# One 128-feature group of a down-projection: the moving operand of 288 columns split into two of 144, each with its own weight load

## The chip, the cores and the metric

The kernel runs on one core of a Trainium2 chip. The metric is the device time of one execution in microseconds (us); lower is better. Before the change three runs took 1708.25, 1707.87 and 1704.91 us: a median of 1707.87 us.

Names used below: PE is TensorE's matmul stream, PEld its weight loads (a record LDWEIGHTS for every record MATMUL), DVE is VectorE, ACT is ScalarE, POOL is GpSimd, SP is the SyncE queue that starts the weight transfers. The weights are the stationary operand of a matmul, the activations the moving one; "288 columns" is the width of the moving operand, and so of the output row in PSUM.

## The reference, cut to what matters

The reference is one layer of a decoder: a combined input projection, a gated convolution, a gated delta rule, an output projection with a layer norm, then a feed-forward block with a second layer norm. The change lies in the last product of the feed-forward block:

```
hid = jnp.square(jax.nn.relu(x @ w_up))          # 2048 -> 8192 features
x = layer_norm(ALPHA * x + hid @ w_down, ln2_g, ln2_b)   # 8192 -> 2048
```

There are 256 prompt tokens and 8 x 4 sample tokens, 288 in all. They are handled together: everything is kept with the features on the 128 partitions and the 288 tokens along the free dimension.

## The kernel before, in words

**Products.** All weights and activations are fp32. Each is split into a high and a low part of type float32r, and a product is three matmuls into the same PSUM columns: high weights by high activations (line 206), high weights by low activations (line 207), low weights by high activations (line 208). Each of the three comes with a load of a 128x128 tile of weights, and then streams 288 columns. Line 207 uses the same weights as line 206 and still has its own load.

**Groups and blocks.** `add_group` lists the work as groups of output features. A group is normally 256 features (two tiles of 128), and is cut into blocks of 4 x 128 rows by 256 columns of weights, 512 KB. A block passes four stages: `load` starts its transfer on SP, `split_hi` (ACT, line 179) makes the high part, `split_lo` (DVE, line 186, recorded as line 140) the low part, and `matmuls` issues its 24 matmuls on PE. The main loop at the end of the kernel goes through the blocks in order. In the step of block i it makes the high and the low part of block i + 3, runs what is due at i (the list `due`, filled by `at`), issues the matmuls of block i and starts the transfer of block i + 7. The order of each engine's queue is the order of this code.

**The end of the program.** The feed-forward block goes through four chunks of 2048 hidden features: eight groups of `w_up`, then the groups of `w_down` whose products are added into the residual `acc` in SBUF. In the last chunk the last 256 output features are two groups of 128 (`cols=P`, so that a block holds 8 x 128 rows by 128 columns, and a group of 16 row tiles is two blocks):

- the next-to-last group, features 1792 to 1919: 2 blocks, 16 row tiles, 48 matmuls. `next_to_last` adds its result to `acc` in the step of the block that follows, `collect` one block later transposes it (`turned(14)`, line 608) and gathers the layer norm's statistics of 15 of the 16 feature tiles;
- the last group, features 1920 to 2047: also 48 matmuls. Then `final` adds the result, turns the last tile, finishes the statistics, and writes the output.

Around them on PE stand transposes of finished tiles (`out_tiles` and `turned`, line 608), put there by `at`: four ahead of the last group's first block, two ahead of its second.

The matmul's `start` flag marks the first matmul that writes a PSUM bank; the accumulation of a group lies in one bank.

Of the kernel before, what the change touches and what calls it, by code (L numbers as in the profile page):

```python
# [16 lines left out]
P = 128  # L17
D = 2048
NP_ = 256
NS = 32  # L20
NT = NP_ + NS
NX = NT + 2
KT = D // P
# [10 lines left out]
GW = 256  # L34
# [69 lines left out]
def hybrid_kernel(ctx: ExitStack, tc: tile.TileContext, A):  # L104
# [15 lines left out]
    def nm(s):  # L120
        counter[0] += 1
        return f"{s}{counter[0]}"
# [13 lines left out]
    act, dve, pe, gps, sp = nc.scalar, nc.vector, nc.tensor, nc.gpsimd, nc.sync  # L136
# [11 lines left out]
    w_in = A["w_in"][0]  # L148
    blocks = []

    def add_group(W, col0, row0, nk, acts, evac, width=NT, cols=GW):
        kb = KB * GW // cols
        gi = dict(W=W, col0=col0, acts=acts, evac=evac, width=width, cols=cols, kb=kb)
        for j in range(nk // kb):
            blocks.append((gi, row0 + j * kb * P, j * kb, j == 0, j == nk // kb - 1))

# [4 lines left out]
    def at(i, f):  # L161
        due.setdefault(i, []).append(f)
# [25 lines left out]
    def matmuls(i):  # L188
        gi, r0, k0, first, last = blocks[i]
        if first:  # L190
            gi["ps"] = acp.tile([P, 2, 512], F32, tag="acc", name=nm("acc"))
        ps = gi["ps"]
        h, l = his.pop(i), los.pop(i)
        ah, al = gi["acts"]()
        n = gi["width"]
        kb = gi["kb"]
        h, l = (u.rearrange("p k c -> p (k c)").rearrange("p (k c) -> p k c", k=kb) for u in (h, l))
        for k in range(kb):
            for t in range(gi["cols"] // P):
                o = ps[:, t, 0:n]  # L200
                wh = h[:, k, t * P:(t + 1) * P]
                wl = l[:, k, t * P:(t + 1) * P]
                xh_, xl_ = ah[:, k0 + k, 0:n], al[:, k0 + k, 0:n]
                st = first and k == 0
                en = last and k == kb - 1
                pe.matmul(o, wh, xh_, start=st, stop=False)  # L206
                pe.matmul(o, wh, xl_, start=False, stop=False)  # L207
                pe.matmul(o, wl, xh_, start=False, stop=en)  # L208
                if fill:
                    fill.pop(0)()  # L210
        if last:
            for n, f in enumerate(gi["evac"]):
                at(i + 1 + n, lambda f=f: f(ps))
# [83 lines left out]
    for G in range(2):  # L297
        mark["kqv", G] = len(blocks)
        for sec, c0 in ((1, C_K), (0, C_Q), (2, C_V)):
            for p in range(2):  # L300
                add_group(w_in, c0 + 512 * G + GW * p, 0, KT, acts_x, conv_evac(sec, G, p))
        mark["kqv_end", G] = len(blocks)
# [46 lines left out]
    for p in range(4):  # L349
        add_group(w_in, C_H + GW * p, 0, KT, acts_x, h_evac(p))  # L350
        add_group(w_in, C_GC + GW * p, 0, KT, acts_x, gc_evac(p))
        add_group(w_in, C_GB + GW * p, 0, KT, acts_x, gb_evac(p))
# [399 lines left out]
    for c in range(4):  # L752
# [4 lines left out]
        acts_h = lambda: (ph["hh"], ph["hl"])  # L757
        for p in range(8 if c < 3 else 7):
            add_group(A["w_down"][0], GW * p, 2048 * c, KT, acts_h, down_evac(c, p))

    add_group(A["w_down"][0], D - 2 * P, 3 * 2048, KT, acts_h, [next_to_last, collect], cols=P)
    add_group(A["w_down"][0], D - P, 3 * 2048, KT, acts_h, [final], cols=P)


# [574 lines left out]
    t = raw.pop(0)  # L1339
# [16 lines left out]
    for i in range(3):  # L1356
        split_hi(i + 1, 2)
        split_lo(i + 1, 2)
        load(i + 5)
        fill.extend(lambda k=k: x_tile(k) for k in range(4 * i + 4, 4 * i + 8))  # L1360
        matmuls(i)
# [9 lines left out]
    for i in range(3, len(blocks)):  # L1371
# [47 lines left out]
        if i == mark["down3"] - 60:  # L1419
            tail_consts()  # L1420
        matmuls(i)
        load(i + AHEAD + 4)
    for i in sorted(due):
# [31 lines left out]
```

## Time and profile before

| | |
|---|---|
| device time, median of 3 runs | 1707.87 us (1704.91 to 1708.25) |
| profiled execution: span from its first to its last instruction | 1703.4 us |
| difference of the median and that span | 4.5 us |
| PE busy / weight loads busy | 1688.5 us / 1668.7 us, 13063 records each |
| DVE / ACT / POOL busy | 1007.2 / 734.1 / 133.8 us |
| matmuls of 288 columns by 128x128 float32r weights: busy, mean | 295 to 300 ns |
| their weight loads: busy, mean | 188 to 189 ns |

The page gives the profiled execution's span and no other time of it; what lies around the span is told only by the 4.5 us to the median of the runs.

How to read it: matmuls are pipelined, so that the "busy" duration of one (295 ns) is its way through the array and not what it costs. What it costs is the distance from its start to the start of the next. In the rows of a timeline the first number is the start in us from the begin of the span, the second the duration in us of the row (of all of its instructions from the first start to the last end, where "x4" or "x16" stands at the end), then engine, source line, operation, output and inputs, the tile (128*128 is a weight tile of 128 rows and 128 columns) and the moving operand.

### The profile page before, as it was taken

How to read it: one execution, taken by the hardware profiler on the slowest of the kernel's cores; microseconds unless marked ns; L12 is line 12 of the kernel's file. 1: busy time of each engine (PE TensorE's matmuls, PEld its weight loads, DVE VectorE, ACT ScalarE, POOL GpSimd, SP SyncE). 2: the span in 40 equal slices, each digit the busy share in tenths (PEclk: the TensorE clock that was granted, in tenths of full speed). 3: DMA queues.
4: the chain of work that ended last, by engine and by line, in shares of the span. 5: the costliest groups of instructions: out<-in, count | busy, mean ns of one | idle time of the engine just before them, and what ended most of it. 6: DMA issues, size and time to landing. Idle time of an engine off the chain costs nothing.

```text
span 1703.4 us, 31106 instructions
## 1 busy us (share of the span) xinstructions
PE 1688.5 (99%) x13063; PEld 1668.7 (98%) x13063; DVE 1007.2 (59%) x1296; ACT 734.1 (43%) x1067; POOL 133.8 (8%) x223
## 2 busy tenths in 40 slices
PE   9999999999999999999999999999999999999997
PEld 7999999999999999999999999999999999999997
DVE  5577876758544444456778844566445654466565
ACT  4675626333543333334445533444334433344442
POOL 2232412023300000000010000000000000000000
PEclk9999999999999999999999999999999999999999
DMA  8464456435555555555565555555555555555552
GB/s 244 140 194 139 123 175 200 150 115 180 162 170 169 166 162 170 163 164 165 158 190 174 165 170 161 164 170 162 167 168 161 163 171 162 164 167 164 162 162 80
DMA packets 275097, 279.18 MB, mean 164 GB/s; under 512 B 13131, under 2 KB 270092, under 8 KB 274952
## 3 DMA queue, kind: packets, MB, share of 16 engines
q1 hardware_dynamic: 270414, 265.95, 51.3%
q0 software_dynamic: 4256, 11.12, 2.3%
q8 instruction: 102, 1.67, 0.4%
q14 instruction: 37, 0.30, 0.1%
q10 hardware_dynamic: 288, 0.13, 0.0%
HBM read 269.68 MB, written 7.48 MB: 163 GB/s over the span
## 4 chain that ended last, share of the span: by engine, by line
PE 98%; DVE 1%; DMA 0%; POOL 0%; issue 0%; SPq 0%; ACT 0%; POOLq 0%; ACTq 0%
PE acc L206 31%; PE acc L208 31%; PE acc L207 31%; PE g L1084 1%; DMA xr<-in_x_prompt_dram 0%; PE g L1072 0%; PE g L1231 0%; PE g L1251 0%; PE g L831 0%; DVE w L143 0%; PE g L1254 0%; PE g L1203 0%; PE g L1243 0%; PE g L608 0%; PE g L798 0%; PE g L958 0%
## 5 line engine op out<-in xcount | busy, mean ns | idle before, releaser
L140 DVE TENSOR_TENSOR lo<-raw,hi 128x1024 fp32r<-128x1024 f32 (+2 forms) x502 | 614.0, 1226 | 556.2 <-ACT hi L179 553.7
L179 ACT CAST hi<-raw 128x1024 fp32r<-128x1024 f32 (+1 forms) x498 | 517.6, 1041 | 765.0 <-PE acc L207 707.7
L206 PE MATMUL acc<-xh,hi 128*128 128x288 f32 x1408 | 422.9, 300 | 0.0
L208 PE MATMUL acc<-xh,lo 128*128 128x288 f32 x1408 | 416.7, 296 | 0.0
L207 PE MATMUL acc<-xl,hi 128*128 128x288 f32 x1408 | 416.5, 296 | 0.0
L206 PE MATMUL acc<-dh,hi 128*128 128x290 f32 x1024 | 303.9, 297 | 0.0
L207 PE MATMUL acc<-dl,hi 128*128 128x290 f32 x1024 | 303.3, 296 | 0.0
L208 PE MATMUL acc<-dh,lo 128*128 128x290 f32 x1024 | 302.7, 296 | 0.0
L206 PE MATMUL acc<-hh,hi 128*128 128x288 f32 x1024 | 302.3, 295 | 0.0
L208 PE MATMUL acc<-hh,lo 128*128 128x288 f32 x1024 | 302.3, 295 | 0.0
L207 PE MATMUL acc<-hl,hi 128*128 128x288 f32 x1024 | 302.3, 295 | 0.0
L206 PEld LDWEIGHTS acc<-xh,hi 128*128 128x128 f32 x1408 | 265.4, 189 | 2.6 <-issue 0.7
L207 PEld LDWEIGHTS acc<-xl,hi 128*128 128x128 f32 x1408 | 265.8, 189 | 0.5
L208 PEld LDWEIGHTS acc<-xh,lo 128*128 128x128 f32 x1408 | 265.6, 189 | 0.0
L206 PEld LDWEIGHTS acc<-dh,hi 128*128 128x128 f32 x1024 | 193.6, 189 | 0.1
L208 PEld LDWEIGHTS acc<-dh,lo 128*128 128x128 f32 x1024 | 193.3, 189 | 0.0
L207 PEld LDWEIGHTS acc<-dl,hi 128*128 128x128 f32 x1024 | 193.3, 189 | 0.1
L207 PEld LDWEIGHTS acc<-hl,hi 128*128 128x128 f32 x1024 | 192.5, 188 | 0.0
L208 PEld LDWEIGHTS acc<-hh,lo 128*128 128x128 f32 x1024 | 192.3, 188 | 0.0
L206 PEld LDWEIGHTS acc<-hh,hi 128*128 128x128 f32 x1024 | 192.1, 188 | 0.0
L207 PE MATMUL acc<-ml,hi 128*128 128x288 f32 x256 | 75.6, 295 | 0.0
L208 PE MATMUL acc<-mh,lo 128*128 128x288 f32 x256 | 75.6, 295 | 0.0
(404 smaller groups left out, 1620.0 us busy)
## 6 DMA issues: line engine op xcount, KB each, us to landing
raw<-in_w_in_dram SPq DMA_DIRECT2D x176, 512.0 KB, 3.5
raw<-in_w_up_dram SPq DMA_DIRECT2D x128, 512.0 KB, 3.9
raw<-in_w_down_dram SPq DMA_DIRECT2D x128, 512.0 KB, 3.7
raw<-in_w_o_dram SPq DMA_DIRECT2D x32, 512.0 KB, 3.7
raw<-in_w_a_out_dram SPq DMA_DIRECT2D x16, 512.0 KB, 3.7
raw<-in_w_b_out_dram SPq DMA_DIRECT2D x16, 512.0 KB, 3.6
S<-in_state_gdn_dram POOLq DMA_DIRECT2D x8, 512.0 KB, 7.8
out_dram<-S POOLq DMA_DIRECT2D x8, 512.0 KB, 4.9
```

The source lines that it names most:

```text
L140: dve.tensor_tensor(out=out, in0=a, in1=b, op=op)
L179: act.copy(his[i][:, k:k + step], raw[i][:, k:k + step])
L206: pe.matmul(o, wh, xh_, start=st, stop=False)
L207: pe.matmul(o, wh, xl_, start=False, stop=False)
L208: pe.matmul(o, wl, xh_, start=False, stop=en)
L1084: pe.matmul(out[r, q * 64:q * 64 + 64], a[r, q, :], b[r, q, :], start=True, stop=True)
```

## The change

`add_group` gets an argument `parts`, kept with the group. `matmuls` runs the three matmuls of a weight tile once for each part, over a slice of the 288 columns. All groups have `parts=1`, one part of 288 columns as before, and only the next-to-last group has `parts=2`: columns 0 to 143 first, all three matmuls, then columns 144 to 287. So its 48 matmuls of 288 columns become 96 of 144, and its weight loads 96 instead of 48. The `start` flag is set on the very first matmul of the group alone, whose bank holds both halves. `skip_group_check=True` tells the builder not to check the nesting of the flags; it adds no instruction.

```diff
-    def add_group(W, col0, row0, nk, acts, evac, width=NT, cols=GW):
+    def add_group(W, col0, row0, nk, acts, evac, width=NT, cols=GW, parts=1):
...
-                o = ps[:, t, 0:n]
                 wh = h[:, k, t * P:(t + 1) * P]
                 wl = l[:, k, t * P:(t + 1) * P]
-                xh_, xl_ = ah[:, k0 + k, 0:n], al[:, k0 + k, 0:n]
-                st = first and k == 0
                 en = last and k == kb - 1
-                pe.matmul(o, wh, xh_, start=st, stop=False)
-                pe.matmul(o, wh, xl_, start=False, stop=False)
-                pe.matmul(o, wl, xh_, start=False, stop=en)
+                for u in range(gi["parts"]):
+                    cs = slice(u * n // gi["parts"], (u + 1) * n // gi["parts"])
+                    o = ps[:, t, cs]
+                    xh_, xl_ = ah[:, k0 + k, cs], al[:, k0 + k, cs]
+                    st = first and k == 0 and u == 0
+                    pe.matmul(o, wh, xh_, start=st, stop=False, skip_group_check=True)
+                    pe.matmul(o, wh, xl_, start=False, stop=False, skip_group_check=True)
+                    pe.matmul(o, wl, xh_, start=False, stop=en, skip_group_check=True)
...
-    add_group(A["w_down"][0], D - 2 * P, 3 * 2048, KT, acts_h, [next_to_last, collect], cols=P)
+    add_group(A["w_down"][0], D - 2 * P, 3 * 2048, KT, acts_h, [next_to_last, collect], cols=P, parts=2)
```

The changed code is two lines longer above the functions that follow, so lines 206, 207, 208 and 608 are 208, 209, 210 and 610 after it. The instructions of DVE, ACT, POOL and SP, and their order, are the same; PE's are the same outside this group.

The first place is PE's queue where the group begins: the last two matmuls of the group before (acc2038), and the first of the next-to-last group (acc2051). hh and hl are the high and low activations, hi and lo the parts of a weight block. Before:

```order
L207 MATMUL acc2038_17553<-hl1832_15784,hi2036_17548 128x288
L208 MATMUL acc2038_17553<-hh1831_15783,lo2037_17550 128x288
L206 MATMUL acc2051_17686<-hh1831_15783,hi2040_17580 128x288 [waits PE_49]
L207 MATMUL acc2051_17686<-hl1832_15784,hi2040_17580 128x288
L208 MATMUL acc2051_17686<-hh1831_15783,lo2041_17582 128x288 [waits DVE_49]
L206 MATMUL acc2051_17686<-hh1831_15783,hi2040_17580 128x288
```

And after the change:

```order
L209 MATMUL acc2038_17553<-hl1832_15784,hi2036_17548 128x288
L210 MATMUL acc2038_17553<-hh1831_15783,lo2037_17550 128x288
L208 MATMUL acc2051_17686<-hh1831_15783,hi2040_17580 128x144 [waits PE_49]
L209 MATMUL acc2051_17686<-hl1832_15784,hi2040_17580 128x144
L210 MATMUL acc2051_17686<-hh1831_15783,lo2041_17582 128x144 [waits DVE_49]
L208 MATMUL acc2051_17686<-hh1831_15783,hi2040_17580 128x144
```

The matmuls are half as wide, the waits stand at the same two, and the sixth row is no longer the next row tile but the second half of the first.

The second place is PE's queue where the group ends: its last matmuls, the four transposes of finished tiles (g2052, g2053) and the first matmul of the last group (acc2054). Before:

```order
L208 MATMUL acc2051_17686<-hh1831_15783,lo2043_17610 128x288
L608 MATMUL g2052_17735<-cf_75,acc_9588 128x128 [waits DVE_49]
L608 MATMUL g2052_17735<-cf_75,acc_9588 128x128
L608 MATMUL g2053_17741<-cf_75,acc_9588 128x128 x2
L206 MATMUL acc2054_17748<-hh1831_15783,hi2046_17649 128x288 [waits PE_49,Activation_49]
```

And after the change:

```order
L210 MATMUL acc2051_17686<-hh1831_15783,lo2043_17610 128x144
L610 MATMUL g2052_17783<-cf_75,acc_9588 128x128 [waits DVE_49]
L610 MATMUL g2052_17783<-cf_75,acc_9588 128x128
L610 MATMUL g2053_17789<-cf_75,acc_9588 128x128 x2
L208 MATMUL acc2054_17796<-hh1831_15783,hi2046_17649 128x288 [waits PE_49,Activation_49]
```

What follows the group is the same, with the same waits, 48 instructions later.

More of the change, by code (lines that the diff above doesn't have):

```diff
@@ L149, in hybrid_kernel @@
     blocks = []
-    def add_group(W, col0, row0, nk, acts, evac, width=NT, cols=GW):
+    def add_group(W, col0, row0, nk, acts, evac, width=NT, cols=GW, parts=1):
         kb = KB * GW // cols
-        gi = dict(W=W, col0=col0, acts=acts, evac=evac, width=width, cols=cols, kb=kb)
+        gi = dict(W=W, col0=col0, acts=acts, evac=evac, width=width, cols=cols, kb=kb, parts=parts)
         for j in range(nk // kb):
```

## The prediction

> **What bounds the kernel now.** I read the page first: the span, the row of each engine, the clock, and the shares of the chain that ended last.
>
> ```profile
> span 1703.4 us, 31106 instructions
> PE 1688.5 (99%) x13063; PEld 1668.7 (98%) x13063; DVE 1007.2 (59%) x1296; ACT 734.1 (43%) x1067; POOL 133.8 (8%) x223
> ...
> PEclk9999999999999999999999999999999999999999
> ...
> PE 98%; DVE 1%; DMA 0%; POOL 0%; issue 0%; SPq 0%; ACT 0%; POOLq 0%; ACTq 0%
> ```
>
> TensorE is the bound: 98% of the chain, at the full clock. Both of its rows, streams and loads, are nearly full, so the rows do not say which of the two limits. That is read from the distances between starts in the timeline. This is PE where the group begins and ends.
>
> ```profile
> 1674.49 0.30 PE L208 MATMUL acc<-hh,lo 128*128 128x288 f32 x1
> 1674.63 0.29 PE L206 MATMUL acc<-hh,hi 128*128 128x288 f32 x1
> ...
> 1680.89 0.29 PE L208 MATMUL acc<-hh,lo 128*128 128x288 f32 x1
> 1681.02 0.60 PE L608 MATMUL g<-cf,acc 128*128 128x128 f32 x4
> ```
>
> The group is the 48 matmuls from 1674.63 to 1681.02 (the four transposes at 1681.02 are the row of line 608 that follows it in the queue): 6.39 us, 0.1331 us each, without a gap. The busy time of that stretch, by engine (PE, PEld, DVE, ACT, POOL, then clock and DMA share):
>
> ```profile
> 1674.63:1681.02 6.39, 6.39 (x50) 6.39 (x49) 1.89 (x2) 1.25 (x3) 0.00 (x0) 1.00 0.01 3
> ```
>
> DVE and ACT work 1.89 and 1.25 us of it, the DMA share is 0.01: all weights are there. The chain behind the last matmul of the program, from the chain in order of time:
>
> ```profile
> 1688.09 0.15 PE acc L208
> 1688.26 0.43 DVE acc L140
> 1688.74 0.45 PE g L608 x2
> ...
> 1697.16 1.30 POOLq L1451
> ```
>
> It hangs on the last matmul of the last group (1688.09). Whatever the group adds on PE moves this end by as much.
>
> **The change, part by part.** What it removes: 48 matmuls of 288 columns, 6.39 us. What it adds: 96 matmuls of 144 columns and 96 loads of 128x128 weights. Nothing moves on another engine. No row of the trace has a float32r matmul of 144 columns, so its price comes from two separate ones: what 144 columns take to stream, and what a load takes when the stream no longer covers it. The larger of the two is the distance.
>
> The stream first. Two matmuls of 512 columns (line 997), the next matmul behind them, and sixteen of 288 columns over weights of only 32 columns (line 831), with the matmul behind them:
>
> ```profile
> 300.43 0.63 PE L997 MATMUL g<-glx,hmr 128*128 128x512 f32 x2
> 300.90 0.29 PE L206 MATMUL acc<-xh,hi 128*128 128x288 f32 x1
> ...
> 45.13 2.27 PE L831 MATMUL g<-xh,wba 128*32 128x288 f32 x16
> 47.23 0.30 PE L206 MATMUL acc<-xh,hi 128*128 128x288 f32 x1
> ```
>
> 512 columns take (300.90 - 300.43) / 2 = 0.235 us, 0.459 ns a column; 288 columns take 0.1331, 0.462 ns a column. With a quarter of the weights to load, 288 columns still take (47.23 - 45.13) / 16 = 0.131. So today the stream sets the distance and the load lies under it. 144 columns at 0.462 ns are 0.0665 us.
>
> The load next. In the gates there is a run of matmuls with full 128x128 weights and streams of 8 to 64 columns, too short to cover anything (loads first, then three of their streams):
>
> ```profile
> 72.25 0.30 PEld L873 LDWEIGHTS g<-be,ao 128*128 128x128 f32 x2
> 72.48 0.30 PEld L874 LDWEIGHTS g<-g,cf 128*128 128x128 f32 x2
> 72.70 0.30 PEld L875 LDWEIGHTS g<-gm,cf 128*128 128x128 f32 x2
> 72.92 0.30 PEld L876 LDWEIGHTS g<-be,ao 128*128 128x128 f32 x2
> 73.15 0.30 PEld L877 LDWEIGHTS g<-be,ao 128*128 128x128 f32 x2
> 73.37 0.30 PEld L878 LDWEIGHTS g<-be,ao 128*128 128x128 f32 x2
> 73.59 0.19 PEld L206 LDWEIGHTS acc<-xh,hi 128*128 128x128 f32 x1
> 73.70 0.19 PEld L207 LDWEIGHTS acc<-xl,hi 128*128 128x128 f32 x1
> ...
> 72.28 0.37 PE L873 MATMUL g<-be,ao 128*128 128x16 f32 x2
> 72.73 0.41 PE L875 MATMUL g<-gm,cf 128*128 128x64 f32 x2
> 73.17 0.37 PE L877 MATMUL g<-be,ao 128*128 128x8 f32 x2
> ```
>
> Twelve loads from 72.25 to 73.59: 1.34 us, 0.1117 each, whether 8 or 64 columns stream. These weights are plain fp32. That float32r weights cost the same is seen at the two loads behind them: the one of line 206 starts at 73.59 and the next at 73.70, 0.11 later. The same stands where the last group begins, behind the transposes:
>
> ```profile
> 1681.35 0.19 PEld L206 LDWEIGHTS acc<-hh,hi 128*128 128x128 f32 x1
> 1681.46 0.19 PEld L207 LDWEIGHTS acc<-hl,hi 128*128 128x128 f32 x1
> 1681.60 0.19 PEld L208 LDWEIGHTS acc<-hh,lo 128*128 128x128 f32 x1
> ```
>
> There the first load found a short stream ahead of it and held the next up by 0.11; the one after it found a stream of 288 columns, and the distance was the usual 0.14. The durations agree, from the groups by line and shape (the last numbers before the second bar are the total and the mean in ns):
>
> ```profile
> L831 PEld LDWEIGHTS g<-xh,wba 128*32 128x32 f32 x16 | 1.7, 108 | 0.4
> ...
> L206 PEld LDWEIGHTS acc<-hh,hi 128*128 128x128 f32 x1024 | 192.1, 188 | 0.0
> L207 PEld LDWEIGHTS acc<-hl,hi 128*128 128x128 f32 x1024 | 192.5, 188 | 0.0
> ```
>
> 32 columns of float32r weights take 108 ns, 128 take 188: 80 ns for 96 columns, 0.83 ns a column, 107 ns for 128. The rest is latency that two loads share. The last two rows also show that line 207 loads weights that are already in the array, 1024 times of 1024: nothing drops a repeated load, so the second half's loads are paid too.
>
> The sum: 0.1117 is larger than 0.0665, so the load sets the distance. 96 x 0.1117 = 10.72 us in place of 6.39: **+4.33 us**. On the path that sets the end all of it is paid, since PE has no gap in the group or behind it that could take it up. From 1703.4 the span goes to 1707.7; the median stands 4.5 above that span, and I carry the difference over: 1707.87 + 4.33 = **1712.2 us**.
>
> Bounds of the distance: not below the stream, 0.0665, which gives 96 x 0.0665 = 6.38 and no change (a gain is excluded, since the columns streamed stay 13824; at 0.459 ns a column it would be 0.05 us). Above, with the load as long as today's distance, 0.1331: 12.78, +6.39 us. I take 0.1117, as it comes from loads of the same size under streams that cannot cover them.
>
> The Trainium skill, "TensorE: Matmul & The Clock Gate", section "LDWEIGHTS (loading the stationary operand)", gives the load as its columns divided by 1.2 GHz, 106.7 ns for 128. By that rule the group would take 96 x 0.1067 = 10.24 us, +3.85 instead of the row's +4.33. The row's 0.1117 is 5 ns longer than the rule; the trace agrees on the slope and decides on the size.
>
> Edits that cost nothing: the flags and the unchecked nesting add no instruction. The adds and transposes of finished tiles on DVE and PE come later by what PE loses; they have the last group's matmuls as cover. On DVE:
>
> ```profile
> 1681.44 0.50 DVE L610 BATCH_NORM_STATS2 r<-g 128x6 f32<-128x128 f32 x2 [3.73 <-PE g L608]
> ...
> 1685.08 0.50 DVE L610 BATCH_NORM_STATS2 r<-g 128x6 f32<-128x128 f32 x2 [1.72 <-PE g L608]
> ```
>
> DVE waits 3.73 and 1.72 us for PE around the group's end, never PE for DVE; a later PE lengthens these waits and nothing else. If that cover were gone, the 0.50 us rows would show on the path.
>
> **The rivals.**
>
> *Hidden: not slower.* The next weights are fetched while two short streams run, a second load starting before the first is in use, and the stream's 0.0665 sets the distance: 1707.9 us. For it: today's loads start a whole matmul ahead of their streams. Against it: the run at 72.25 had nothing to do but load, and still took 0.1117 each; the queue was full of loads there too. It decides if the loads' distance falls under 0.067. Chance 0.07.
>
> *Half hidden.* Only part of the load is exposed, with a distance midway between 0.0665 and 0.1117, 0.089: 8.54 us, +2.15, 1710.0 us. Against it, again, the 0.1117 for all widths from 8 to 64. The Trainium skill, same page, section "Back-to-back issue gap", measures about 81 ns for a load and a matmul of 128 columns in a stream of pairs; with 16 more columns by the 0.462 ns above, an estimate of 88 ns, +2.1 us. None of the rows above with 128x128 weights is as quick. Chance 0.07.
>
> *In turn.* Load and stream do not overlap in this pattern: 0.1117 + 0.0665 = 0.178, 17.1 us, +10.7, 1718.6 us. Against it: today 0.1331 holds a load of 0.11 and a stream of 0.133, so they overlap. The skill's page says, in "Part 3: Packing small matmuls — row/col tiling", that loads overlap matmuls in flight only with other row groups, which would mean this. The trace contradicts it in every row of the group, as all use 128 rows. Chance 0.06, with other costs above the forecast. A slower clock, because PE streams less of the time, would be one of these; in the run of short streams it stayed at 1.00 (the number behind POOL's in the row of that stretch):
>
> ```profile
> 72.00:73.60 1.60, 1.60 (x17) 1.60 (x16) 1.53 (x4) 1.58 (x3) 0.21 (x1) 1.00 0.98 317
> ```
>
> **How the numbers follow.** The forecast, a distance of 0.105 to 0.12, has 0.80. A measurement of this kernel can tell about 0.2% from no change, 3.42 us. The forecast lies 0.91 us above that, and the three runs before spread over 3.34, so the forecast alone gives "slower" in some 0.72 of its cases: 0.58. With "in turn" (0.06) and a little of "half hidden" that is 0.65. Faster has no mechanism, only the runs' spread: 0.02. Within 0.2%: 0.33.
>
> The range: at the bottom the rival without a change at today's median, 1707.8; at the top the bound of 0.1331 on the highest run, 1708.25 + 6.39 = 1714.6. What it leaves out is "in turn" and the tails of the spread, some 0.17.
>
> **What would show it.** In the profile after: 96 rows of 128x144 in the group, starts 0.11 apart on both PE and PEld, the group 10.7 us long, the chain from the last matmul to the end 15.3 us (1703.4 - 1688.1) as now, the clock row still full. Starts 0.067 apart would prove the first rival, 0.178 the third. The prediction is wrong if the group is 10.7 us long and the time has not followed, or if the group is shorter than 9.6 us.

## The result, and the profile after

| | before | after |
|---|---|---|
| device time, median | 1706.70 us (18 runs, 1704.91 to 1708.69) | 1711.03 us (18 runs, 1709.20 to 1713.52) |
| span of the profiled execution | 1703.4 us | 1707.8 us |
| the next-to-last group on PE | 6.39 us | 10.67 us |

The ratio is 1.0025, with a 95% interval of [1.0018, 1.0032]: slower by 4.33 us between the medians. Part of the spread lies outside the change: of the 18 runs after, the four with the lowest mean granted clock (0.991) took 1712.56 to 1713.52 us, the other fourteen 1709.20 to 1711.76. The page of the profile after, the same rows as before:

```profile
span 1707.8 us, 31202 instructions
...
PE 1693.1 (99%) x13111; PEld 1673.0 (98%) x13111; DVE 1007.5 (59%) x1296; ACT 734.6 (43%) x1067; POOL 134.1 (8%) x223
...
PEclk9999999999999999999999999999999999999999
```

48 matmuls and 48 loads more (13111 for 13063), both rows as full as before, the clock the same. Nothing here says where the 4.4 us of the span went; the distances in the timeline do. PE, from the last 288-column matmul ahead of the group to the transposes behind it:

```profile
1674.61 0.30 PE L210 MATMUL acc<-hh,lo 128*128 128x288 f32 x1
1674.74 0.23 PE L208 MATMUL acc<-hh,hi 128*128 128x144 f32 x1
1674.81 0.27 PE L209 MATMUL acc<-hl,hi 128*128 128x144 f32 x1
1674.91 0.28 PE L210 MATMUL acc<-hh,lo 128*128 128x144 f32 x1
...
1685.30 0.28 PE L210 MATMUL acc<-hh,lo 128*128 128x144 f32 x1
1685.41 0.61 PE L610 MATMUL g<-cf,acc 128*128 128x128 f32 x4
```

And its weight loads:

```profile
1674.61 0.19 PEld L208 LDWEIGHTS acc<-hh,hi 128*128 128x128 f32 x1
1674.74 0.19 PEld L209 LDWEIGHTS acc<-hl,hi 128*128 128x128 f32 x1
1674.85 0.19 PEld L210 LDWEIGHTS acc<-hh,lo 128*128 128x128 f32 x1
...
1685.23 0.19 PEld L210 LDWEIGHTS acc<-hh,lo 128*128 128x128 f32 x1
```

The distances between the loads hold the whole argument. The row of a matmul stands 0.06 to 0.07 us behind the row of its load (1674.74 and 1674.81, 1685.23 and 1685.30), which is what 144 columns take to stream; that is not what sets the pace. The loads start 0.11 apart from 1674.74 to 1685.23 (94 distances, 10.49 us, 0.1116 each), and from the second matmul on the matmuls start as far apart as they do. The group takes 10.67 us (1685.41 - 1674.74). The busy time of that stretch, with clock and DMA share behind the five engines:

```profile
1674.74:1685.41 10.67, 10.67 (x98) 10.67 (x97) 1.89 (x2) 1.25 (x3) 0.00 (x0) 1.00 0.01 2
```

DVE and ACT do the same 1.89 and 1.25 us of work in it as before. Behind the group the span is as long as it was: 1707.8 - 1685.41 = 22.39 us, before 1703.4 - 1681.02 = 22.38. DVE's waits around the end of the group:

```profile
1685.85 0.50 DVE L612 BATCH_NORM_STATS2 r<-g 128x6 f32<-128x128 f32 x2 [8.03 <-PE g L610]
...
1689.48 0.50 DVE L612 BATCH_NORM_STATS2 r<-g 128x6 f32<-128x128 f32 x2 [1.73 <-PE g L610]
```

The first wait for PE has grown from 3.73 to 8.03 us, by the 4.3 that PE lost; the second is as it was.

### The profile page after: what moved, and what is told of

Its sections match the earlier page's. It is cut to its first block, busy times and chain, and to the rows that moved or that the text cites. A ratio compares the mean times of both kernels' runs of the same rounds, so it can differ in the third digit from the quotient of the medians.

```text
span 1707.8 us, 31202 instructions
## 1 busy us (share of the span) xinstructions
PE 1693.1 (99%) x13111; PEld 1673.0 (98%) x13111; DVE 1007.5 (59%) x1296; ACT 734.6 (43%) x1067; POOL 134.1 (8%) x223
## 4 chain that ended last, share of the span: by engine, by line
PE 98%; DVE 1%; DMA 0%; POOL 0%; issue 0%; SPq 0%; ACT 0%; POOLq 0%; ACTq 0%
PE acc L208 31%; PE acc L210 31%; PE acc L209 31%; PE g L1086 1%; DMA xr<-in_x_prompt_dram 0%; PE g L1074 0%; PE g L1233 0%; PE g L1253 0%; PE g L833 0%; DVE w L143 0%; PE g L1256 0%; PE g L1205 0%; PE g L610 0%; PE g L1245 0%; PE g L800 0%; PE g L960 0%
## 5 line engine op out<-in xcount | busy, mean ns | idle before, releaser
L209 PE MATMUL acc<-hl,hi 128*128 128x288 f32 (+1 forms) x1040 | 306.4, 295 | 0.0
L210 PE MATMUL acc<-hh,lo 128*128 128x288 f32 (+1 forms) x1040 | 306.4, 295 | 0.0
L208 PE MATMUL acc<-hh,hi 128*128 128x288 f32 (+1 forms) x1040 | 306.3, 295 | 0.0
```

The costliest lines, as they stand in the source:

```text
L208: pe.matmul(o, wh, xh_, start=st, stop=False, skip_group_check=True)
L209: pe.matmul(o, wh, xl_, start=False, stop=False, skip_group_check=True)
L210: pe.matmul(o, wl, xh_, start=False, stop=en, skip_group_check=True)
```

## The experiments

All kernels start from the changed one. Theory A is the prediction's: the distance between two matmuls is the larger of the stream (0.462 ns a column) and the load of the next weights (0.1117 us for 128 columns). Theory B: a matmul has a fixed cost of its own, whatever it loads, some 0.09 us. Theory C: the change of the output columns costs.

### Half the weights: e1_weights64

```diff
-                wh = h[:, k, t * P:(t + 1) * P]
-                wl = l[:, k, t * P:(t + 1) * P]
+                mw = 64 if gi["parts"] > 1 else P
+                wh = h[:, k, t * P:t * P + mw]
+                wl = l[:, k, t * P:t * P + mw]
...
-                    o = ps[:, t, cs]
+                    o = ps[0:mw, t, cs]
...
-        tt(a, a, ps[:, 0, 0:NT], ADD)
+        tt(a[0:64], a[0:64], ps[0:64, 0, 0:NT], ADD)
```

> The split group loads only 64 of its 128 weight columns and leaves out output features 1856 to 1919; as many matmuls, loads and streamed columns as in the changed kernel. Theory A (the load sets the distance; 0.83 ns a weight column): a load takes some 0.058 us, the stream of 144 columns 0.0665 covers it, the 96 matmuls take 6.4 us, and the time is that of before, 1706.7 us, 4.3 under the changed kernel. Theory B (a fixed cost of each further matmul, about 0.09 us, whatever it loads): starts 0.11 apart as in the changed kernel, 10.7 us, 1711.0.

Measured: 1706.71 us (11 runs) beside 1706.15 for before, ratio 1.0004 [0.9995, 1.0013]. PE in this kernel, where a weight tile reads 128*64:

```profile
1675.43 0.23 PE L209 MATMUL acc<-hh,hi 128*64 128x144 f32 x1
1675.50 0.23 PE L210 MATMUL acc<-hl,hi 128*64 128x144 f32 x1
1675.56 0.23 PE L211 MATMUL acc<-hh,lo 128*64 128x144 f32 x1
...
1681.93 0.61 PE L611 MATMUL g<-cf,acc 128*128 128x128 f32 x4
```

The same 96 matmuls of 144 columns with 96 loads take 6.50 us (1681.93 - 1675.43), 0.0677 each, in place of 10.67. The only thing that was made smaller on PE is the weight tile, and with it the rows of the output that it makes. B is dead: the further matmuls, their issue and the halves together cost no more than 0.11 us (6.50 for the 6.39 of before); the length of the load does.

### Shorter loads, shorter streams: e7_weights64_four72

e1, and besides:

```diff
-    add_group(A["w_down"][0], D - 2 * P, 3 * 2048, KT, acts_h, [next_to_last, collect], cols=P, parts=2)
+    add_group(A["w_down"][0], D - 2 * P, 3 * 2048, KT, acts_h, [next_to_last, collect], cols=P, parts=4)
```

> Weights of 64 columns (output features 1856 to 1919 are left out) and four parts of 72 columns, so that the stream, 0.033 us, no longer covers the shorter load. Theory A: the distance is the load of 64 columns, about 0.058 us, 192 of them 11.1 us. Theory B: 0.100 apart, 19.2 us, as with full weights.

Measured: 1709.86 us in one run; the group, by the row of its stretch:

```profile
1674.50:1685.67 11.17, 11.17 (x195) 11.17 (x193) 1.89 (x2) 1.25 (x3) 0.00 (x0) 1.00 0.01 3
```

192 matmuls in 11.17 us, 0.0582 each; A had 11.1. With streams of 0.033 the load of 64 columns is bare. Beside the changed kernel there are now two bare loads, 0.0582 for 64 columns and 0.1116 for 128: 0.83 ns a column and some 5 ns besides.

### Wide and narrow: e2_256_32

```diff
-                    cs = slice(u * n // gi["parts"], (u + 1) * n // gi["parts"])
+                    cs = slice(0, n) if gi["parts"] == 1 else (slice(0, NP_), slice(NP_, n))[u]
```

> Split into 256 and 32 columns instead of 144 and 144. Theory A: a matmul of 256 columns takes its stream, 256 x 0.462 ns = 0.118 us, which covers the next load; one of 32 columns takes the next load, 0.112: 48 x 0.230 = 11.0 us. Theory B, by the line 0.0893 us and 0.152 ns a column: 0.128 and 0.094, 48 x 0.222 = 10.7 us, with the wide ones well over their stream.

Measured: 1710.67 us in one run. The loads of this kernel, from the second one of the group on, and the transposes' loads behind it:

```profile
1675.51 0.19 PEld L209 LDWEIGHTS acc<-hl,hi 128*128 128x128 f32 x1
1675.62 0.19 PEld L210 LDWEIGHTS acc<-hh,lo 128*128 128x128 f32 x1
1675.74 0.19 PEld L208 LDWEIGHTS acc<-hh,hi 128*128 128x128 f32 x1
1675.86 0.19 PEld L209 LDWEIGHTS acc<-hl,hi 128*128 128x128 f32 x1
1675.97 0.19 PEld L210 LDWEIGHTS acc<-hh,lo 128*128 128x128 f32 x1
...
1686.46 0.20 PEld L610 LDWEIGHTS g<-cf,acc 128*128 128x128 f32 x2
```

The three distances under 256 columns are 0.11, 0.12, 0.12, the one under 32 columns that follows 0.11. A had 0.118 and 0.112, B 0.128 and 0.094: the last one speaks for A. From the first row to the last, the whole group but its first load, it is 10.95 us (1686.46 - 1675.51), between A's 11.0 and B's 10.7 and close to A.

### The halves apart: e4_halves_outer

```diff
-        for k in range(kb):
+        for u, k in [(u, k) for u in range(gi["parts"]) for k in range(kb)]:
             for t in range(gi["cols"] // P):
...
-                for u in range(gi["parts"]):
```

> The same 96 matmuls, but in each block all matmuls of the first 144 columns come before all of the second, so that the half changes once a block instead of every three matmuls. Theory A: starts 0.11 apart, 10.7 us, as the loads are the same. Theory C (it is the change of the output columns that costs, 47 changes of some 0.09 us): about 6.5 us.

Measured: 1713.52 us in one run, a span of 1711.7. The row of the group's stretch:

```profile
1677.93:1688.60 10.67, 10.67 (x98) 10.67 (x97) 1.89 (x2) 1.25 (x3) 0.00 (x0) 1.00 0.01 2
```

10.67 us, to the hundredth what the changed kernel takes: theory C is out. That this one run is 2.5 us over the changed kernel's median is not the group's doing: the group begins 3.2 us later here (1677.93 for 1674.74), so the difference was there ahead of it. The granted clock shows where: between 9 and 24 us it was 0.57 here and 1.00 in the changed kernel's trace, between 210 and 230 us 0.83 and 1.00.

### Elsewhere, and more of it: e6_last_group and e5_chunk

```diff
-    add_group(A["w_down"][0], D - 2 * P, 3 * 2048, KT, acts_h, [next_to_last, collect], cols=P, parts=2)
-    add_group(A["w_down"][0], D - P, 3 * 2048, KT, acts_h, [final], cols=P)
+    add_group(A["w_down"][0], D - 2 * P, 3 * 2048, KT, acts_h, [next_to_last, collect], cols=P)
+    add_group(A["w_down"][0], D - P, 3 * 2048, KT, acts_h, [final], cols=P, parts=2)
```

> The last group is split instead of the next-to-last. Theory A: the next-to-last group takes 6.4 us, the last one's two blocks 10.7 us, and the time is that of the changed kernel, 4.3 over before, 1711.0 us. If the place counted (the transposes and adds of finished tiles as cover), it would come out more than 1 us away from that.

Measured: 1713.16 us (7 runs) beside 1706.67 for before, ratio 1.0032 [1.0020, 1.0043]. The interval holds the 1.0025 of the changed kernel, but the median lies 2.2 us above A's 1711.0, so by its own words ("more than 1 us") the expectation missed. The trace says whether the place is the reason. The next-to-last group is short again, from the first row to the second 6.40 us:

```profile
1675.62 0.29 PE L208 MATMUL acc<-hh,hi 128*128 128x288 f32 x1
...
1682.02 0.60 PE L610 MATMUL g<-cf,acc 128*128 128x128 f32 x4
```

Behind it lie 1708.6 - 1682.02 = 26.58 us, in the kernel before 22.38: the split costs 4.20 us in the last group, where it cost 10.67 - 6.39 = 4.28 in the next-to-last. So the place makes no difference of 1 us. The span is 0.8 us above the changed kernel's because the next-to-last group began 0.9 us later; between 9 and 24 us the granted clock was 0.67 here and 1.00 there. The median is high for the same reason: four of these seven runs have the mean clock of 0.991, of the changed kernel's eighteen also four; the other three took 1710.38 to 1711.34 us, A's 1711.0 within 0.7.

For e5 every group of the last chunk gets two parts:

```diff
-            add_group(A["w_down"][0], GW * p, 2048 * c, KT, acts_h, down_evac(c, p))
+            add_group(A["w_down"][0], GW * p, 2048 * c, KT, acts_h, down_evac(c, p), parts=2 if c == 3 else 1)
...
-    add_group(A["w_down"][0], D - P, 3 * 2048, KT, acts_h, [final], cols=P)
+    add_group(A["w_down"][0], D - P, 3 * 2048, KT, acts_h, [final], cols=P, parts=2)
```

> All nine groups of the last chunk of the down-projection in two halves: 768 matmuls of 288 become 1536 of 144, sixteen times the change. Theory A, with nothing to take it up anywhere: 768 x (2 x 0.1117 - 0.1331) = 69.4 us over before, 1776.1 us, ratio 1.0407. If part of the added time were taken up by waits around the group, the gain per group would be smaller in the other groups or the ratio below 1.03.

Measured: 1775.45 us beside 1706.67, ratio 1.0399 [1.0384, 1.0413]: 68.8 us for the 69.4 of A. The cost is 16 times that of one group, so over the nine groups it is paid in full. Most of that stretch, by engine:

```profile
1582.53:1750.00 167.47, 167.47 (x1506) 167.47 (x1504) 59.67 (x94) 38.07 (x50) 0.10 (x1) 1.00 0.27 83
```

### Four parts, and the clock: e3_four72

```diff
-    add_group(A["w_down"][0], D - 2 * P, 3 * 2048, KT, acts_h, [next_to_last, collect], cols=P, parts=2)
+    add_group(A["w_down"][0], D - 2 * P, 3 * 2048, KT, acts_h, [next_to_last, collect], cols=P, parts=4)
```

> Four parts of 72 columns, 192 matmuls and 192 loads. Theory A: the distance stays at the load's 0.1117, 192 x 0.1117 = 21.4 us, 15.1 over before: 1721.8 us, ratio 1.0088. Theory B, with a line through the two measured distances (0.1331 at 288 columns, 0.1112 at 144: 0.0893 us and 0.152 ns a column): 0.100 apart, 19.2 us, 12.9 over before: 1719.6.

Measured: 1738.03 us (5 runs) beside 1706.15, ratio 1.0191 [1.0178, 1.0205]: 31.9 us over before, where A had 15.1 and B 12.9. Both missed. Two stretches of the group (clock in the third column from the end), and the loads at the seam:

```profile
1675.63:1681.57 5.94, 5.94 (x56) 5.94 (x55) 1.89 (x2) 1.25 (x3) 0.00 (x0) 1.00 0.01 3
1681.57:1711.01 29.44, 29.44 (x141) 29.44 (x140) 0.00 (x0) 0.00 (x0) 0.00 (x0) 0.50 0.00 1
```

```profile
1681.43 0.19 PEld L210 LDWEIGHTS acc<-hh,lo 128*128 128x128 f32 x1
1681.55 0.29 PEld L208 LDWEIGHTS acc<-hh,hi 128*128 128x128 f32 x1
1681.71 0.34 PEld L209 LDWEIGHTS acc<-hl,hi 128*128 128x128 f32 x1
1681.93 0.33 PEld L210 LDWEIGHTS acc<-hh,lo 128*128 128x128 f32 x1
1682.14 0.33 PEld L208 LDWEIGHTS acc<-hh,hi 128*128 128x128 f32 x1
```

For 5.94 us the distance is A's 0.112. Then the granted clock falls to 0.50 and the loads stand 0.21 apart. PE is as "busy" as ever, 5.94 of 5.94 and 29.44 of 29.44. What is new is the share of the time in which columns stream: 0.033 of 0.112 us, 30%, against 0.0665 of 0.112, 60%, in the changed kernel. e7 streams the same 72 columns in as many matmuls but 0.033 of 0.058, 57%, and its clock stayed at 1.00 (its row above): neither the number nor the width of the matmuls decides by itself, and the share fits all three. e7's weight tile is half as wide, a second difference. The four runs that follow vary the share under full weights, where it changes together with the width; that it is the share and not the width rests on e7.

### How little streaming is too little: f1_three96, f2_three96_chunk, f3_six48

f1 has three parts in the next-to-last group:

```diff
-    add_group(A["w_down"][0], D - 2 * P, 3 * 2048, KT, acts_h, [next_to_last, collect], cols=P, parts=2)
+    add_group(A["w_down"][0], D - 2 * P, 3 * 2048, KT, acts_h, [next_to_last, collect], cols=P, parts=3)
```

f2 is e5 with three parts in place of two in all nine groups. f3 is f1 with six parts.

> The next-to-last group in three parts of 96 columns, 144 matmuls. With four parts of 72 columns the granted clock fell to 0.50 some 6 us into the group, where the array streamed 0.033 of every 0.112 us (30%); with two parts (0.0665 of 0.112, 60%) it stayed at 1.00. Three parts stream 0.044 of 0.112, 40%. Theory G1 (the clock falls only below a share under 40%): 144 x 0.1117 = 16.1 us at the full clock, 9.7 over before. Theory G2 (40% is too little already): half the clock after 6 us, loads 0.213 apart, about 5.9 + 91 x 0.213 = 25.3 us, 18.9 over before.

> All nine groups of the last chunk in three parts of 96 columns: the 40% of streaming for over 250 us instead of 16. G1: 768 x (3 x 0.1117 - 0.1331) = 155 us over before, clock 1.00 throughout. G2, or a clock that falls only after longer than one group: up to 768 x (3 x 0.213 - 0.1331) = 389 us over before, with the clock at 0.50 in the last sixth of the span.

> The next-to-last group in six parts of 48 columns, 288 matmuls: 0.022 of every 0.112 us streams, 20%. If the clock follows the share of time in which the array streams, it falls as with four parts, after some 6 us: 5.9 + 235 x 0.213 = 56 us, 49.6 over before. At the full clock it would be 288 x 0.1117 = 32.2 us.

Measured: f1 1728.73 us (4 runs) beside 1706.72, ratio 1.0126 [1.0109, 1.0143], 22.0 us over before; f2 2096.88 and f3 1758.82 us in one run each, 390.2 and 52.1 over. The clock in stretches of f1, where the last row is the last group:

```profile
1677.49:1683.50 6.01, 6.01 (x57) 6.01 (x55) 1.89 (x2) 1.25 (x3) 0.00 (x0) 1.00 0.01 3
1684.00:1702.40 18.40, 18.40 (x88) 18.40 (x88) 0.00 (x0) 0.00 (x0) 0.00 (x0) 0.50 0.00 1
1702.56:1706.00 3.44, 3.44 (x16) 3.44 (x17) 1.91 (x7) 0.00 (x0) 0.00 (x0) 0.50 0.00 0
```

Of f2:

```profile
1585.87:1592.20 6.33, 6.33 (x60) 6.33 (x58) 3.60 (x5) 2.07 (x4) 0.10 (x1) 1.00 0.63 174
1593.00:2078.00 485.00, 484.80 (x2277) 484.64 (x2277) 58.12 (x96) 35.94 (x46) 0.00 (x0) 0.50 0.08 27
```

And of f3:

```profile
1675.80:1681.50 5.70, 5.70 (x54) 5.70 (x53) 1.89 (x2) 1.25 (x3) 0.00 (x0) 1.00 0.01 3
1682.00:1731.70 49.70, 49.70 (x235) 49.70 (x234) 0.00 (x0) 0.00 (x0) 0.00 (x0) 0.50 0.00 1
```

G2 holds: at 40% the clock falls some 6 us into the group, as at 30% and at 20%, and in f2 it stays down for 485 us. f1's group takes 25.07 us (the seam with the last group is at 1702.56), where G2 had 25.3. Behind it lie 1727.8 - 1702.56 = 25.24 us for 22.38 before: 2.9 us more are lost in the last group, which still begins at half the clock (third row). f2's 390.2 us are the 389 that were worked out for half the clock; f3's 52.1 are 2.5 above its 49.6, and its last group begins at half the clock as well.

### When the clock comes back: f4_four72_then_two

```diff
+        np_ = gi["parts"] if k0 == 0 else min(gi["parts"], 2)
...
-                for u in range(gi["parts"]):
-                    cs = slice(u * n // gi["parts"], (u + 1) * n // gi["parts"])
+                for u in range(np_):
+                    cs = slice(u * n // np_, (u + 1) * n // np_)
...
-    add_group(A["w_down"][0], D - 2 * P, 3 * 2048, KT, acts_h, [next_to_last, collect], cols=P, parts=2)
+    add_group(A["w_down"][0], D - 2 * P, 3 * 2048, KT, acts_h, [next_to_last, collect], cols=P, parts=4)
```

> Four parts of 72 columns in the group's first block only, two parts of 144 in its second: 96 matmuls of 72, then 48 of 144. The clock should fall some 6 us into the first block (53 matmuls at 0.112, then 43 at 0.213, 15.1 us). In the second block, at half the clock, a stream of 144 columns takes 0.133 of 0.213 us, 62%. If it is the share of streaming that gates the clock, it comes back to 1.00 within some 6 us of the second block, about 28 matmuls, and the group takes some 15.1 + 6.0 + 2.2 = 23.3 us; if the clock only comes back when the streaming is near full, the second block stays at 0.213, 10.2 us, and the group takes 25.3.

Measured: 1725.63 us in one run. The first block at the full and at half the clock, the second block (144 columns), and the last group's begin:

```profile
1675.49:1681.50 6.01, 6.01 (x57) 6.01 (x55) 1.89 (x2) 1.25 (x3) 0.00 (x0) 1.00 0.01 3
1682.00:1690.30 8.30, 8.30 (x41) 8.30 (x40) 0.00 (x0) 0.00 (x0) 0.00 (x0) 0.50 0.00 0
1690.30:1700.50 10.20, 10.20 (x49) 10.20 (x50) 0.00 (x0) 0.00 (x0) 0.00 (x0) 0.50 0.01 2
1700.60:1702.50 1.90, 1.90 (x11) 1.90 (x11) 1.28 (x6) 0.00 (x0) 0.00 (x0) 0.61 0.00 0
1703.00:1706.00 3.00, 3.00 (x25) 3.00 (x24) 0.81 (x4) 0.00 (x0) 0.00 (x0) 1.00 0.00 0
```

The second block stays at 0.50 for its whole 10.2 us; the group takes about 25.1 us, as the second case had it. The clock returns within 2 us of the last group's first 288-column matmul (1701.26). But the 62% of the expectation are too many: it took 0.133 us for 144 columns, twice the 0.0665. Two matmuls of 288 columns at half the clock, in the last group of f4, start 0.24 us apart:

```profile
1701.65 0.44 PE L210 MATMUL acc<-hl,hi 128*128 128x288 f32 x1
1701.89 0.38 PE L211 MATMUL acc<-hh,lo 128*128 128x288 f32 x1
```

So 144 columns stream some 0.12 of every 0.213 us, 56%. That share did not bring the clock back in 10.2 us. e7 kept it at 57% and the changed kernel at 60%; whether the clock needs more to come back than to stay is left open, as no run streamed 60% from the lower clock.

## Why the prediction was right

Point by point, in the prediction's order:

- **The load sets the distance.** Right, 0.1116 us for a forecast of 0.1117, and the group 10.67 us for 10.72. Shown by e1 (half the weights: 6.50 us, the time of before) and e7 (the bare load of 64 columns, 0.0582).
- **The stream of 144 columns, 0.0665.** Right: 0.0677 over the whole of e1, where the stream sets the distance.
- **Repeated loads are not dropped.** Right: 13111 loads for 13111 matmuls.
- **All of it is on the path.** Right: 22.39 us behind the group for 22.38 before, and 68.8 us for sixteen times the work in e5.
- **Nothing else costs.** Right: DVE's one wait grew by PE's 4.3 us, and no new wait appeared; e4 shows that changing the halves is free.
- **The sum.** +4.33 us was forecast and 4.33 lies between the medians. That they agree to the hundredth is luck: the group grew by 4.28 us in the traces and the span by 4.4, and the interval of the ratio is worth 3.1 to 5.5 us. The time itself was put 1.2 us too high, 1712.2 for 1711.03: the three runs of before had a median of 1707.87, and eighteen have 1706.70. The step that missed is the carrying over of that median, not a term of the sum. Nor are the 4.5 us between that median and the span of before a fixed amount around the span: each of the 18 runs after took 1.7 to 1.9 us more than its own span, and the 4.5 set the trace of one run beside the median of others.
- **The rivals.** "Hidden" and "half hidden" needed distances of 0.067 and 0.089, "in turn" 0.178; the loads stand at 0.1116. The Trainium skill's rule for a load ("TensorE: Matmul & The Clock Gate", "LDWEIGHTS (loading the stationary operand)"), 106.7 ns, is 5 ns short of it. For 64 columns the rule makes an estimate of 53.3 ns, and e7 has 58.2.
- **The clock.** The prediction named a slower clock as one of the other costs, and argued against it from the run of short streams at 72 us, where it stayed at 1.00. The conclusion held for two parts, but the argument did not carry it, and that part was luck: that run lasts 1.6 us, and in e3 and f1 to f4 the clock fell only after some 6 us. Three parts brought 22.0 us (f1), where this way of adding up gives 144 x 0.1117 - 6.39 = 9.7.

## What to carry to other kernels

Price a matmul by the distance between starts, as the larger of its stream and the next load of weights, and take both from runs of the trace in which the other cannot set it. In this kernel the two meet at 0.1117 us / 0.462 ns = 242 columns. That crossing is worked out, not measured: against a 128-column weight tile 144 columns paid for the load, 256 (e2) and 288 hid it. And look at the granted clock before trusting such a sum for streams that are much narrower: a full PE row does not show that the array is streaming.

## What the runs showed of the hardware

- The clock is lost without a gap on PE. With columns streaming 20%, 30% or 40% of the time it fell from 1.00 to 0.50 after about 6 us (5.94 us in e3, between 6.0 and 6.5 in f1); at 57% (e7, with weights of half the width) and 60% it stayed, in e5 for more than 167 us. Where between 40% and 57% it turns was not measured. The Trainium skill ("TensorE: Matmul & The Clock Gate", "What's actually happening") says that the gate follows PE's recent activity and has these two levels; the levels agree with the rows, and the rows add that loads alone do not count as enough activity.
- At half the clock both terms grow: the loads stand 0.213 us apart in e3 for 0.112, 1.9 times, and matmuls of 288 columns 0.24 in f4 for 0.133, 1.8 times.
- Once down, the clock did not come back at 56% streaming (f4, 10.2 us), and came back within 2 us under streams of 288 columns. In f1 that took about 4 us: these streams begin at 1703.31, and the clock is 0.50 up to 1707 and 1.00 from 1708. What sets this delay is not shown.
- The clock also differs between runs far ahead of the group. Behind a wait of PE for DVE of 3.00 us, at 217 us, the stretch from 210 to 230 us has a clock of 0.83 in e4 and of 1.00 in the changed kernel, where the wait is as long. Why is not shown.
